# Second matrix of the second SwiGLU by seven block products, with operand sums made during the first matrix

## Chip, core and metric

The kernel runs on one core of one Trainium2 chip. The metric is the device time of one execution in microseconds, as the median of several runs.

## What is computed

The reference is a two-layer diffusion trunk: 1024 latent tokens and 256 context tokens of width 1024, a Fourier mixer in the first layer, differential attention in the second, and a SwiGLU behind each. Only the last SwiGLU is touched, over the 1024 latent tokens, all in float32:

```python
def swiglu(h, w_in, w_out):
    gate, up = jnp.split(h @ w_in, 2, axis=-1)
    return (jax.nn.silu(gate) * up) @ w_out

x = x + g2 * swiglu(modulate(rms_norm(x, norm_gain[i, 1]), sh2, sc2), ffn_w_in[i], ffn_w_out[i])
```

`w_in` is 1024 x 5632 (gate and up, 2816 columns each), `w_out` 2816 x 1024.

## The kernel before

Every float32 matmul is made of three in the float32r format: high times high, high times low and low times high (`mm3`, lines 49 to 52, or `prod`, lines 1447 to 1452). The operands are split beforehand: ScalarE copies the high part (line 55) and VectorE subtracts it for the low part (line 56). One such split of 128 x 512 numbers is called a unit.

The last SwiGLU has two stages.

The first matrix (lines 1369 to 1585) goes over the 2816 columns in 22 rows f of 128. Each row makes gate and up for both halves of the tokens (g = 0 and 1, 512 tokens each) from seven products instead of eight, numbered 1, 2, 5, 6, 3, 7, 4. A product is 4 x 3 matmuls of 128 x 128 by 128 x 512 into one PSUM bank. The order of the products is `seq`; from row 3 on a row's product 3 comes between products 6 and 7 of the next row. `load` fetches the weight columns of a row through SP's DMA queue, nine products ahead in the text (LEADL). `prep` makes the weight sums on GpSimd (lines 1435 to 1441) and splits them into units, four ahead (LEADP); there are six unit buffers. `evac` reads the banks out: line 1471 (ScalarE copies a bank), 1479 (VectorE adds the second product to the gate), 1480 and 1493 (silu on ScalarE), 1488, 1491 and 1497 (further VectorE sums with a bank). `act_out` multiplies gate and up on GpSimd (line 1463) in place in one of ten buffers e, writes the 128 x 512 result to `aD` in DRAM and frees both buffers.

The second matrix (lines 1588 to 1662) makes the output transposed: for each half g of the tokens eight banks, one for each 128 columns of `w_out`, take 22 steps f of 8 x 3 matmuls. `prep_down` loads a row of `w_out` (512 KB) and a half row of `aD` (256 KB) and splits both. Two steps are prepared during the first matrix (`load_first`, `prep_first`). In the last six steps of a half (TAIL) the loop runs bank by bank, so that a bank is finished, scaled and added to the residual `xt` on VectorE (line 1654) while the others still accumulate. `store` transposes finished columns on TensorE (line 1617), copies them out of PSUM through buffers o (line 1620) and writes them to the output. The residual halves are loaded from DRAM at lines 1598 and 1599; the tile xt0 has been used for weight columns of the first rows before.

The text gives each engine's operations in an order and with buffers by name; the program builder sets the waits and may move an operation ahead of others on its engine where its inputs and buffers allow it.

## Time and profile before

| | us |
|---|---|
| median of 3 runs | 2753.19 (2752.32 to 2753.29) |
| the profiled execution | 2754.87 |
| its span, first to last instruction | 2753.1 |
| first matrix of the last SwiGLU, first matmul to last | 2068 to 2500 |
| second matrix, first matmul to last | 2500 to 2747 |

The profile is of one execution. Engines: PE is TensorE's matmuls, PEld its weight loads, DVE is VectorE, ACT ScalarE, POOL GpSimd, SP the queue that issues the DMAs. L12 is line 12 of the kernel. Durations of matmuls overlap, so a matmul's price is the distance from one start to the next. In a timeline row stand the start, the duration, engine, line, operation, what it writes and reads, and in brackets how long the engine was idle before it and what ended that.

### The profile page before, as it was taken

Reading aid. Unit: us, or ns where it says so; the run is one execution under the profiler, and the core shown is the slowest. Engines: PE = TensorE matmul, PEld = TensorE weight load, DVE = VectorE, ACT = ScalarE, POOL = GpSimd, SP = SyncE. Lnnn points to the kernel's source line nnn. Section 1 sums busy time; section 2 is a strip of 40 time slices with the busy share of each in tenths; the row PEclk is TensorE's granted clock in tenths of the full one; section 3 lists DMA queues with packets and bytes.
Section 4 is the critical chain, followed back from the end, with each engine's and each line's share of the span. In section 5 each row is a group of like instructions: output and inputs, shape, how many; then the busy total and the mean of one; then the engine's idle time right before and its main releaser. Section 6 shows DMA issues by size and latency. Waiting matters only on the chain. (4 is left out here: it accounts for less than half of the span.)

```text
span 2753.1 us, 35789 instructions
## 1 busy us (share of the span) xinstructions
PE 2658.3 (97%) x13242; PEld 2185.4 (79%) x13242; DVE 1544.1 (56%) x2867; ACT 1118.4 (41%) x1954; POOL 952.1 (35%) x786
## 2 busy tenths in 40 slices
PE   6999999999999999999999899998988999999999
PEld 3678888888888888878888677787776788888887
DVE  6744535443344343485776597898458555554242
ACT  4643333323232111242444488898444333334131
POOL 4332023312121000022333287888145666651000
PEclk9999999999999999999999999999999999999999
DMA  6583122223232111133344632423243323226352
GB/s 213 190 270 100 39 62 82 88 74 95 73 96 70 39 35 43 53 105 105 115 146 144 197 105 70 123 85 100 81 137 107 103 73 88 73 85 214 103 184 88
DMA packets 288641, 292.75 MB, mean 106 GB/s; under 512 B 16313, under 2 KB 206034, under 8 KB 288466
## 3 DMA queue, kind: packets, MB, share of 16 engines
q1 hardware_dynamic: 286306, 286.79, 33.7%
q0 software_dynamic: 2160, 3.67, 0.4%
q8 instruction: 104, 1.70, 0.3%
q14 instruction: 71, 0.58, 0.1%
HBM read 236.93 MB, written 53.48 MB: 105 GB/s over the span
## 5 line engine op out<-in xcount | busy, mean ns | idle before, releaser
L50 PE MATMUL ps<-un,whl 128*128 128x512 f32 x1184 | 465.1, 394 | 1.4 <-ACT XT L602 1.2
L51 PE MATMUL ps<-un,whl 128*128 128x512 f32 x1184 | 462.1, 390 | 0.2 <-DVE un L56 0.2
L52 PE MATMUL ps<-un,whl 128*128 128x512 f32 x1184 | 461.4, 390 | 0.0
L56 DVE TENSOR_TENSOR whl<-raw,whl 128x512 fp32r<-128x512 f32 x219 | 169.7, 787 | 267.6 <-ACT whl L55 266.5
L50 PEld LDWEIGHTS ps<-un,whl 128*128 128x128 f32 x1184 | 222.7, 188 | 55.1 <-issue 3.5
L52 PEld LDWEIGHTS ps<-un,whl 128*128 128x128 f32 x1184 | 222.7, 188 | 47.1
L51 PEld LDWEIGHTS ps<-un,whl 128*128 128x128 f32 x1184 | 222.9, 188 | 45.1 <-DVE un L56 0.7
L55 ACT ACTIVATE whl<-raw 128x512 fp32r<-128x512 f32 x219 | 134.3, 627 | 243.8 <-PE ps L52 177.9
L746 DVE SCALAR_TENSOR_TENSOR XT<-ps,mods,XT 128x512 f32<-128x512 f32 (+1 forms) x264 | 170.2, 659 | 84.7 <-PE ps L52 84.7
L272 POOL TENSOR_TENSOR acc<-acc,aw 128x512 f32<-128x512 f32 x84 | 113.1, 1346 | 295.0 <-ACT acc L268 231.7
L1051 POOL TENSOR_TENSOR e<-e,e 128x1280 f32<-128x1280 f32 x62 | 183.4, 2961 | 32.1 <-ACT e L1050 29.9
L617 POOL TENSOR_TENSOR nacc<-nacc,s 128x512 f32<-128x512 f32 (+1 forms) x35 | 41.2, 1176 | 416.7 <-ACT s L616 395.2
L1031 ACT ACTIVATE e<-e,st 128x1280 f32<-128x1280 f32 x128 | 175.2, 1372 | 23.6 <-DVE e L1030 22.0
L1029 DVE TENSOR_SCALAR_CACHE_REDUCE e<-sc 128x1024 f32<-128x1024 f32 x128 | 155.3, 1219 | 28.4 <-POOL e L1051 14.1
L51 PE MATMUL ps<-u,whl 128*128 128x256 f32 x592 | 167.5, 283 | 0.0
L52 PE MATMUL ps<-u,whl 128*128 128x256 f32 x592 | 167.4, 283 | 0.0
L50 PE MATMUL ps<-u,whl 128*128 128x256 f32 x592 | 167.3, 283 | 0.0
L829 PE MATMUL ps<-whl,un 128*128 128x512 f32 x384 | 152.7, 398 | 0.0
L830 PE MATMUL ps<-whl,un 128*128 128x512 f32 x384 | 150.3, 392 | 0.9 <-DVE whl L56 0.7
L831 PE MATMUL ps<-whl,un 128*128 128x512 f32 x384 | 149.9, 391 | 0.0
L51 PE MATMUL b<-au,wu 128*128 128x512 f32 x336 | 130.9, 390 | 0.2 <-DVE au L56 0.2
L52 PE MATMUL b<-au,wu 128*128 128x512 f32 x336 | 130.8, 389 | 0.0
(447 smaller groups left out, 6380.5 us busy)
## 6 DMA issues: line engine op xcount, KB each, us to landing
aw<-in_w_ada SPq DMA_DIRECT2D x96, 256.0 KB, 2.8
raw<-in_ffn_w_in SPq DMA_DIRECT2D x88, 256.0 KB, 2.9
wr<-in_ffn_w_out SPq DMA_DIRECT2D x42, 512.0 KB, 3.6
wada<-in_w_ada SPq DMA_DIRECT2D x48, 256.0 KB, 3.2
un<-in_w_ada SPq DMA_DIRECT2D x48, 256.0 KB, 4.6
raw<-in_diff_w_in SPq DMA_DIRECT2D x48, 256.0 KB, 3.5
rq<-in_ffn_w_in SPq DMA_DIRECT2D x24, 512.0 KB, 5.7
raw<-in_ffn_w_out SPq DMA_DIRECT2D x44, 256.0 KB, 2.9
```

The source lines that it names most:

```text
L50: PE.matmul(out, wh, mh, start=start, stop=False)
L51: PE.matmul(out, wh, ml, start=False, stop=False)
L52: PE.matmul(out, wl, mh, start=False, stop=stop)
L55: S.activation(out=hl[:, 0], in_=src, func=AF.Copy)
L56: (lo_eng or V).tensor_tensor(out=hl[:, 1], in0=src, in1=r32(hl[:, 0]), op=ALU.subtract)
L746: V.scalar_tensor_tensor(out=xs, in0=pt, scalar=gmod[c][:, nn:nn + 1], in1=xs, op0=ALU.mult, op1=ALU.add)
L829: PE.matmul(pt, hk[:, 0, tsl], ws[k][:, 0], start=k == 0, stop=False)
L830: PE.matmul(pt, hk[:, 0, tsl], ws[k][:, 1], start=False, stop=False)
L831: PE.matmul(pt, hk[:, 1, tsl], ws[k][:, 0], start=False, stop=k == NC - 1)
L1029: V.tensor_scalar(e[:, 0:L], sc.rearrange("p a b -> p (a b)"), -1.0, 3.0e38, op0=ALU.mult, op1=ALU.min, accum_out=col(c))
L1031: S.activation(out=e, in_=e, func=AF.Exp, scale=-1.0, bias=col(4 + c), accum_out=col(10 + c))
L1051: G.tensor_tensor(out=e0, in0=e0, in1=e1, op=ALU.add)
```

## The change

Rows f of the first matrix are paired: an even row 2i makes row i of the upper half of the 2816, an odd row 2i + 1 row i of the lower half (`row`). So each pair gives four activation blocks, b11 and b12 (upper, both halves of the tokens) and b21 and b22 (lower). The second matrix is now seven products of half size in place of eight, each over 11 rows, four blocks of 128 columns and 512 tokens: 1, 2 and 4 take plain blocks of `w_out`, 3, 5, 6 and 7 sums of them (`sD` in DRAM), and the activations are plain blocks for 1, 2 and 3 and sums for 4 to 7 (`bD`).

The sums are made in `sums`, called by `act_out` when both halves of a row are there: one subtraction on VectorE after an even row, followed by the loads of four blocks of `w_out`; seven additions and subtractions after an odd row, followed by seven DMA writes. From row 4 on `act_out` writes its result into half of the tile xt0 (`side_tile`), not into an e buffer; the weight blocks take the other half. In the first four rows the results stay in e buffers until the pair is done.

The second matrix runs the products in groups (1, 2), (5, 6), (3, 7), (4), with TAIL = 4. `down_evac` spreads each product over the outputs it belongs to. Three units' products, (1, 0), (2, 0) and (1, 1), are prepared in the first matrix. The o buffers are three in place of four, and the last stores are in another order.

```diff
--- before.py
+++ after.py
@@ -1368,8 +1368,15 @@
     ph5.close()
     ph6 = ExitStack()
     wp = ph6.enter_context(tc.tile_pool(name="wp6", bufs=1, reuse_waits="tile"))
-    aD = dram.tile([NF, P, L], F32, name="aD")
+
+    NH = NF // 2
+    bD = {k: dram.tile([NH, P, 512], F32, name=f"bD{k}") for k in (1, 2, 3, 4, 5, 6, 7)}
+    sD = {k: dram.tile([NH, P, 512], F32, name=f"sD{k}") for k in (3, 5, 6, 7)}
     EARLYF, LEADP, LEADL, OWN, NB = 3, 4, 9, 2, 10
+
+    def row(f):
+
+        return f // 2 + NH * (f % 2)
     efree = list(range(NB))
     def eget():
@@ -1391,6 +1398,7 @@
     def wcols(c0):
         return w_in[:, c0:c0 + P].rearrange("(k p) n -> p k n", p=P)
+    w_out = a["ffn_w_out"][1]
     raws, units, again = {}, {}, []
     def load(f, i):
@@ -1398,7 +1406,7 @@
         if i == 1 and f < EARLYF:
             r = wp.tile([P, 1024], F32, name="r4", bufs=2) if f > 1 else \
                 hpool.tile([P, 2, 512], F32, name=f"h{18 + f}").rearrange("p s n -> p (s n)")
-            nc.sync.dma_start(r.rearrange("p (k n) -> p k n", k=NC), wcols(f * P))
+            nc.sync.dma_start(r.rearrange("p (k n) -> p k n", k=NC), wcols(row(f) * P))
             raws[f, "gate"] = r
         elif i == (1 if f >= EARLYF else 5):
             if 0 < f < EARLYF:
@@ -1409,14 +1417,14 @@
                 q = kq.tile([P, 2, 1024], F32, name="rq", tag="q")
                 r = [q[:, j] for j in range(2)]
             for j in range(2):
-                nc.sync.dma_start(r[j].rearrange("p (k n) -> p k n", k=NC), wcols(j * DFF + f * P))
+                nc.sync.dma_start(r[j].rearrange("p (k n) -> p k n", k=NC), wcols(j * DFF + row(f) * P))
             raws[f] = r
         elif i == 3 and 0 < f < EARLYF:
             if f == 1:
                 again.append(xt0_tile())
             r = [again[0][:, 4 * f + 2 * j - 4:4 * f + 2 * j - 2].rearrange("p a n -> p (a n)") for j in range(2)]
             for j in range(2):
-                nc.sync.dma_start(r[j].rearrange("p (k n) -> p k n", k=NC), wcols(j * DFF + f * P))
+                nc.sync.dma_start(r[j].rearrange("p (k n) -> p k n", k=NC), wcols(j * DFF + row(f) * P))
             raws[f, "again"] = r
     def prep(f, i):
@@ -1459,11 +1467,54 @@
             where[f] = bget()
         prod(where[f][1], units.pop((f, i)), held[i], i in (1, 2, 5, 4))
+    acts, side = {}, []
+
+    def side_tile(k):
+        if not side:
+            side.append(xt0_tile())
+        return side[0][:, k]
+
     def act_out(f, g, e, other):
-        G.tensor_tensor(out=e[1], in0=e[1], in1=other[1], op=ALU.mult)
+        i, odd = divmod(f, 2)
+        keep = f < 4
+        dst = e[1] if keep else side_tile(4 + 2 * odd + g)
+        G.tensor_tensor(out=dst, in0=e[1], in1=other[1], op=ALU.mult)
         eput(other)
-        nc.sync.dma_start(aD[f, :, g * 512:(g + 1) * 512], e[1])
-        eput(e)
+        if not keep:
+            eput(e)
+        acts[i, odd, g] = dst, e if keep else None
+        if (odd, g) != (0, 1):
+            nc.sync.dma_start(bD[{(0, 0): 1, (1, 0): 2, (1, 1): 3}[odd, g]][i], dst)
+        if (i, odd, 0) in acts and (i, odd, 1) in acts:
+            sums(i, odd)
+
+    def sums(i, odd):
+
+        def sub(out, in0, in1, op=ALU.subtract):
+            V.tensor_tensor(out=out, in0=in0, in1=in1, op=op)
+
+        x = [side_tile(k) for k in range(4)]
+        b11, b12 = acts[i, 0, 0][0], acts[i, 0, 1][0]
+        if not odd:
+            sub(b11, b12, b11)
+            nc.sync.dma_start(bD[5][i], b11)
+            for k, (r, c) in enumerate(((i, 0), (NH + i, 0), (i, 512), (NH + i, 512))):
+                nc.sync.dma_start(x[k], w_out[r * P:(r + 1) * P, c:c + 512])
+            return
+        b21, b22 = acts[i, 1, 0][0], acts[i, 1, 1][0]
+        sub(b12, b22, b12)
+        sub(b11, b22, b11)
+        sub(b21, b11, b21)
+        sub(x[3], x[2], x[3], ALU.add)
+        sub(x[2], x[0], x[2])
+        sub(x[0], x[3], x[0])
+        sub(x[1], x[1], x[0])
+        for d, ap in ((bD[7], b12), (bD[6], b11), (bD[4], b21), (sD[5], x[3]), (sD[7], x[2]), (sD[6], x[0]), (sD[3], x[1])):
+            nc.sync.dma_start(d[i], ap)
+        for m in range(4):
+            e = acts.pop((i, m // 2, m % 2))[1]
+            if e:
+                eput(e)
     def state(f):
@@ -1534,37 +1585,43 @@
         yield
-    w_out = a["ffn_w_out"][1]
-    FIRST = 2
     ups, drs = {}, {}
-
-    def load_first(f):
-        q = kq.tile([P, 2, 1024], F32, name="rq", tag="q")
-        nc.sync.dma_start(q[:, 0], w_out[f * P:(f + 1) * P, :])
-        nc.sync.dma_start(q[:, 1, 0:512], aD[f, :, 0:512])
-        drs[f] = q
-
-    def prep_first(f):
-        q = drs.pop(f)
-        us = [unit5(OWN) for _ in range(3)]
-        for u, src in zip(us, (q[:, 1, 0:512], q[:, 0, 0:512], q[:, 0, 512:1024])):
-            split(u, src)
-        ups[0, f] = us
+    FIRSTS = [(1, 0), (2, 0), (1, 1)]
+
+    def down_src(k, i):
+
+        r, c = {1: (i, 0), 2: (NH + i, 0), 4: (NH + i, 512)}.get(k, (None, None))
+        return sD[k][i] if r is None else w_out[r * P:(r + 1) * P, c:c + 512], bD[k][i]
+
+    def load_first(k, i):
+        drs[k, i] = [eget(), eget()]
+        for e, src in zip(drs[k, i], down_src(k, i)):
+            nc.sync.dma_start(e[1], src)
+
+    def prep_first(k, i):
+        us = []
+        for e in drs.pop((k, i)):
+            us.append(unit5(OWN))
+            split(us[-1], e[1])
+            eput(e)
+        ups[k, i] = us
     half = second_half()
     next(half)
     nload = nprep = 0
-    todo = seq + [("down", f) for f in range(FIRST)]
+    todo = seq + [("down", ki) for ki in FIRSTS]
     def ahead(n):
         nonlocal nload, nprep
         while nload < min(len(todo), n + LEADL):
             f, i = todo[nload]
-            load_first(i) if f == "down" else load(f, i)
+            if f == "down" and nload >= n + LEADP + 2:
+                break
+            load_first(*i) if f == "down" else load(f, i)
             nload += 1
         while nprep < min(len(todo), n + LEADP):
             f, i = todo[nprep]
-            prep_first(i) if f == "down" else prep(f, i)
+            prep_first(*i) if f == "down" else prep(f, i)
             nprep += 1
     ahead(0)
@@ -1590,24 +1647,27 @@
     psb = ph7.enter_context(tc.tile_pool(name="ps7", bufs=1, space=PSUM, reuse_waits="tile"))
     bfree[:] = range(8)
     out = a["out"].rearrange("o t d -> (o t) d")
-    TAIL = 6
+    TAIL = 4
     xt0 = xt0_tile()
     xt1 = [kq.tile([P, 4, 512], F32, name="xt1", tag="q") for _ in range(2)]
     xt = [xt0, Halves(xt1)]
     for k in range(0, NC, 4):
         nc.sync.dma_start(xt0[:, k:k + 4], x2[:, k:k + 4, 0:512])
         nc.sync.dma_start(xt1[k // 4], x2[:, k:k + 4, 512:1024])
-
-    def prep_down(g, f):
-        raw = wp.tile([P, 1024], F32, name="wr", bufs=3)
-        nc.sync.dma_start(raw, w_out[f * P:(f + 1) * P, :])
-        ar = t2("ar", 3)
-        nc.sync.dma_start(ar, aD[f, :, g * 512:(g + 1) * 512])
-        au = wp.tile([P, 2, 512], F32R, name="au", bufs=8)
-        split(au, ar)
-        w = wp.tile([P, 2, 1024], F32R, name="wu", bufs=6)
-        split(w, raw)
-        ups[g, f] = au, w[:, :, 0:512], w[:, :, 512:1024]
+    gm = mod(1, 0, 5)
+    ngm = wp.tile([P, 32], F32, name="ngm")[:, 0:NC]
+    V.tensor_scalar(ngm, gm, -1.0, None, op0=ALU.mult)
+    uacc = [wp.tile([P, 512], F32, name=f"ua{m}") for m in range(4)]
+
+    def prep_down(k, i):
+        us = []
+        for nm, src in zip(("w", "a"), down_src(k, i)):
+            raw = t2(nm + "r", 4)
+            nc.sync.dma_start(raw, src)
+            u = wp.tile([P, 2, 512], F32R, name=nm + "u", bufs=11)
+            split(u, raw)
+            us.append(u)
+        ups[k, i] = us
     def store(g, k0, k1):
         for j in range(4):
@@ -1615,51 +1675,82 @@
             pb = bget()
             for k in range(k0, k1):
                 PE.transpose(out=pb[1][:, (k - k0) * P:(k - k0 + 1) * P], in_=xt[g][:, k, tsl], identity=ident)
-            o = t2("o", 4)
+            o = t2("o", 3)
             n = (k1 - k0) * P
             (S.copy if j % 2 else V.tensor_copy)(out=o[:, 0:n], in_=pb[1][:, 0:n])
             bput(pb)
             nc.sync.dma_start(out[g * 512 + j * P:g * 512 + (j + 1) * P, k0 * P:k1 * P], o[:, 0:n])
-    stream = [(g, f) for g in range(2) for f in range(NF) if (g, f) not in ups]
+    GROUPS = ((1, 2), (5, 6), (3, 7), (4,))
+    stream = [(k, i) for ks in GROUPS for i in range(NH) for k in ks]
+    stream = [ki for ki in stream if ki not in ups]
     at = 0
     def ahead_down(n):
         nonlocal at
-        while at < min(len(stream), n - FIRST):
+        while at < min(len(stream), n - len(FIRSTS)):
             prep_down(*stream[at])
             at += 1
-    ahead_down(4)
-    for g in range(2):
-        acc = []
-
-        def step(f, nn):
-            au, *ws = ups[g, f]
-            w = ws[nn // 4]
-            nsl = slice((nn % 4) * P, (nn % 4 + 1) * P)
-            mm3(acc[nn][1], w[:, 0, nsl], w[:, 1, nsl], au[:, 0], au[:, 1], f == 0, f == NF - 1)
-
-        for f in range(NF - TAIL):
-            for nn in range(NC):
-                if f == 0:
-                    acc.append(bget())
-                step(f, nn)
-            ahead_down(g * NF + f + 4)
-        ahead_down((g + 1) * NF)
-        for nn in range(NC):
-            for f in range(NF - TAIL, NF):
-                step(f, nn)
-            xs = xt[g][:, nn]
-            V.scalar_tensor_tensor(out=xs, in0=acc[nn][1], scalar=mod(1, 0, 5)[:, nn:nn + 1], in1=xs, op0=ALU.mult, op1=ALU.add)
-            bput(acc[nn])
-            if nn == 1:
-                ahead_down((g + 1) * NF + 3)
-            if g == 1 and nn in (2, 3):
-                store(0, 4 * (nn - 2), 4 * (nn - 1))
-            if g == 1 and nn in (4, 6):
-                store(1, *((0, 4), (4, 6))[nn // 2 - 2])
-    store(1, 6, 8)
+    def add(g, d, src, neg=False):
+        xs = xt[g][:, d]
+        V.scalar_tensor_tensor(out=xs, in0=src, scalar=(ngm if neg else gm)[:, d:d + 1], in1=xs, op0=ALU.mult, op1=ALU.add)
+
+    def down_evac(k, m, pt):
+        u = uacc[m]
+        if k == 1:
+            S.activation(out=u, in_=pt, func=AF.Copy)
+        elif k == 2:
+            add(0, m, pt)
+            add(0, m, u)
+        elif k == 5:
+            add(1, m, pt)
+            add(1, 4 + m, pt)
+        elif k == 6:
+            V.tensor_tensor(out=u, in0=u, in1=pt, op=ALU.add)
+        elif k == 3:
+            add(1, m, pt)
+            add(1, m, u)
+        elif k == 7:
+            V.tensor_tensor(out=u, in0=u, in1=pt, op=ALU.add)
+            add(0, 4 + m, u)
+            add(1, 4 + m, u)
+        else:
+            add(0, 4 + m, pt, neg=True)
+
+    acc = {}
+
+    def step(k, m, i):
+        if i == 0:
+            acc[k, m] = bget()
+        w, au = ups[k, i]
+        nsl = slice(m * P, (m + 1) * P)
+        mm3(acc[k, m][1], w[:, 0, nsl], w[:, 1, nsl], au[:, 0], au[:, 1], i == 0, i == NH - 1)
+
+    base = 0
+    ahead_down(8)
+    for ks in GROUPS:
+        for i in range(NH - TAIL):
+            for k in ks:
+                for m in range(4):
+                    step(k, m, i)
+            ahead_down(base + (i + 1) * len(ks) + 8)
+        for k in ks:
+            for m in range(4):
+                for i in range(NH - TAIL, NH):
+                    step(k, m, i)
+                down_evac(k, m, acc[k, m][1])
+                bput(acc.pop((k, m)))
+                if ks == (4,):
+                    if m in (0, 1):
+                        store(1, 4 * m, 4 * m + 4)
+                    if m == 2:
+                        store(0, 0, 4)
+                    if m == 3:
+                        store(0, 4, 6)
+            ahead_down(base + len(ks) * (NH - TAIL) + 8 + (TAIL * (ks.index(k) + 1)))
+        base += NH * len(ks)
+    store(0, 6, 8)
     ph7.close()
     phq.close()
     up3.close()
```

## Rows read from the trace of the kernel before

**Rows 1.** The page's busy time, share of the span and instructions of TensorE.

```profile
PE 2658.3 (97%) x13242; PEld 2185.4 (79%) x13242; DVE 1544.1 (56%) x2867; ACT 1118.4 (41%) x1954; POOL 952.1 (35%) x786
```

**Rows 2.** Busy time of the engines in three stages, granted clock, DMA share, GB/s.

```profile
core 0: us, PE busy (x) PEld busy (x) DVE busy (x) ACT busy (x) POOL busy (x), PEclk, DMA share, GB/s
...
2150.00:2497.20 347.20, 347.20 (x1513) 283.85 (x1512) 184.39 (x198) 128.71 (x216) 217.45 (x157) 1.00 0.26 78
...
2497.20:2512.00 14.80, 14.72 (x64) 11.63 (x63) 3.97 (x6) 3.48 (x5) 3.01 (x2) 1.00 0.82 288
...
2512.00:2747.30 235.30, 235.11 (x1067) 194.98 (x1066) 91.39 (x108) 69.28 (x90) 0.00 (x0) 1.00 0.44 149
```

**Rows 3.** Timeline of TensorE in the second matrix; and the page's group.

```profile
L51 PE MATMUL b<-au,wu 128*128 128x512 f32 x336 | 130.9, 390 | 0.2 <-DVE au L56 0.2
...
2620.25 0.39 PE L50 MATMUL b<-au,wu 128*128 128x512 f32 x1
...
2630.45 0.39 PE L50 MATMUL b<-au,wu 128*128 128x512 f32 x1
```

**Rows 4.** VectorE in row f's end: a stretch's busy times, and timeline.

```profile
2322.48:2330.09 7.61, 7.61 (x35) 6.28 (x34) 5.18 (x6) 2.38 (x4) 7.45 (x6) 1.00 0.09 34
...
2318.39 0.69 DVE L1491 TENSOR_TENSOR e<-e,b 128x512 f32<-128x512 f32 x1 [0.94 <-PE b L1452]
...
2319.11 0.69 DVE L56 TENSOR_TENSOR whl<-e,whl 128x512 fp32r<-128x512 f32 x1
...
2322.48 1.74 DVE L56 TENSOR_TENSOR whl<-e,whl 128x512 fp32r<-128x512 f32 x1
...
2329.40 0.69 DVE L1479 TENSOR_TENSOR e<-e,b 128x512 f32<-128x512 f32 x1 [0.52 <-PE b L1452]
```

**Rows 5.** Timeline of GpSimd in the same row.

```profile
2321.14 1.28 POOL L1463 TENSOR_TENSOR e<-e,e 128x512 f32<-128x512 f32 x1
...
2323.63 1.74 POOL L1435 TENSOR_TENSOR e<-rq 128x512 f32<-128x512 f32 x1
```

**Rows 6.** Timeline of ScalarE in the same row.

```profile
2330.12 0.63 ACT L1480 ACTIVATE e<-e 128x512 f32<-128x512 f32 x1
...
2334.99 0.60 ACT L1471 ACTIVATE e<-b 128x512 f32<-128x512 f32 x1 [2.10 <-PE b L1452]
```

**Rows 7.** Groups by line, 2150 to 2490: busy us, mean ns, idle before.

```profile
L56 DVE TENSOR_TENSOR wo<-e,wo 128x512 fp32r<-128x512 f32 x45 | 47.9, 1064 | 41.7 <-ACT wo L55 41.2
```

**Rows 8.** First rows: timeline of GpSimd and TensorE, and a stretch's busy times.

```profile
2131.65 1.25 POOL L1463 TENSOR_TENSOR e<-e,e 128x512 f32<-128x512 f32 x1
...
2136.18 0.80 PE L1450 MATMUL b<-h,wo 128*128 128x512 f32 x1 [4.88 <-ACT wo L55]
...
2136.00:2140.00 4.00, 3.82 (x8) 2.65 (x9) 3.84 (x3) 1.69 (x4) 3.92 (x3) 0.50 1.06 350
```

**Rows 9.** Between the matrices: timeline of SP, ScalarE, TensorE; and a DMA issue.

```profile
2121.12 0.37 SPq L1598 DMA_DIRECT2D xt<-x  x1
...
2503.09 0.32 SPq L1465 DMA_DIRECT2D aD<-e  x1
...
2503.45 0.43 SPq L1603 DMA_DIRECT2D wr<-in_ffn_w_out  x1
...
2509.70 1.06 ACT L55 ACTIVATE wu<-wr 128x1024 fp32r<-128x1024 f32 x1 [8.00 <-DMA wr<-in_ffn_w_out]
...
2512.68 0.50 PE L51 MATMUL b<-au,wu 128*128 128x512 f32 x1 [0.19 <-DVE au L56]
...
ar<-aD SPq DMA_DIRECT2D x42, 256.0 KB, 3.6
```

**Rows 10.** The end: TensorE's last matmul; DMA issues, KB each, us to landing.

```profile
2746.84 0.39 PE L52 MATMUL b<-au,wu 128*128 128x512 f32 x1
...
out<-o SPq DMA_DIRECT2D x12, 256.0 KB, 2.5
...
out<-o SPq DMA_DIRECT2D x8, 128.0 KB, 1.8
```

## The prediction

> **What bounds the kernel now.** I began with the page's busy shares: TensorE holds 97% of the span [rows 1], so the question is whether each stage is TensorE's to the last microsecond. The table by stage answers it [rows 2]. In the first matrix's steady part (2150 to 2497.2 us) TensorE is busy 347.20 of 347.20 us while VectorE has 53% and GpSimd 63%. In the second matrix (2512 to 2747.3) it is busy all but 0.2 of 235.3 us, GpSimd does nothing, and the DMA engines are at 44%. So a matmul taken out of the second matrix is worth its full pitch, provided nothing else becomes late. The third view is the timeline, for that pitch and for the slack of the other engines.
>
> A busy time per matmul (390 ns in the page) isn't its price, since matmuls overlap. Start to start, 45 matmuls lie between the two L50 rows: 2630.45 - 2620.25 = 10.20 us, or 0.2267 us each [rows 3].
>
> **Removed: an eighth of the second matrix.** Before: 44 steps (g, f) of 8 x 3 matmuls, 1056 in all (336 per line in the row, three lines, and 48 for the two early steps [rows 3]). After: 7 products x 11 rows x 4 x 3 = 924. That is 132 x 0.2267 = 29.9 us less. The 64 transposes of the stores are the same. Gain: **-29.9 us**.
>
> **Second matrix, the rest of its steady part: 0.** A unit of 12 matmuls lasts 2.72 us. It needs two loads of 256 KB, 524 KB in 2.72 us, or 193 GB/s; now it is 149 on average, and 288 were moved in the busiest stage [rows 2]. Two splits cost VectorE and ScalarE under 1.4 us each (0.69 and about 0.63 a piece [rows 4, 6]). Evictions grow from 16 to 44 VectorE operations, at most three (about 2.25 us) in the 2.72 us of one tail step. A tail holds eight units of eleven, so three are ready when the next group starts, and four more can be prepared in its second half. TensorE hides all that; were the loads to lack a tenth of their time, 77 units would cost 21 us, but the row of 288 speaks against it.
>
> **Added to the first matrix: eight subtractions or additions per pair of rows, on VectorE.** They come as one after an even row and seven in a run after an odd one, as soon as GpSimd has made the second activation (L1463). In capacity there is room: 8 x 0.69 = 5.5 us in the 38.7 us of a pair. What matters is what stands behind the run. GpSimd's product ends at 2322.42 [rows 5]. From 2322.48 to 2330.09, the end of the gate sum L1479, VectorE is busy 5.18 of 7.61 us, so it has 2.43 us to spare [rows 4]. Behind L1479 ScalarE waits for its silu (L1480, 0.63), then does a split (0.63) and the copy of the sixth product (L1471, 0.60, at 2334.99) [rows 6]; the seventh product adds to that bank, one product later. Four products lie between the ends L1491 and L1479 answer to: 11.01 us, 2.75 each [rows 4]. So the copy may end at 2334.99 + 2.75 = 2337.7, L1479 at 2337.7 - 1.86 = 2335.8, which is 5.7 us later than now. With a price p for each of the seven, TensorE is held up by 7p - 2.43 - 5.7. Prices: 0.69 for a split that meets no GpSimd work, 1.74 for one that does [rows 4], 1.064 as the mean of 45 [rows 7]. At 0.69 and 1.064 there is no stall (the second leaves 0.7 us); at 1.74 it is 4.05 us, in nine steady pairs 36 us. GpSimd is busy 7.45 of those 7.61 us [rows 4], so I go a little above the mean, p = 1.23, or 0.48 us a pair: **+4 us (0 to 36)**. Weight units are split some four products ahead, 11 us, and come through a run of 8.6 us. GpSimd gives back what it loses in its idle third.
>
> The row first: beside a GpSimd addition the VectorE split took 1.74 us instead of 0.69, and the GpSimd operation next to it 1.74 instead of 1.28, while VectorE operations with one input in PSUM keep 0.69 [rows 4, 5]. The Trainium skill (SBUF — State Buffer, "Who interferes with whom") has a rule for it: a VectorE instruction with two SBUF inputs and a GpSimd instruction that reads SBUF exclude each other for the whole instruction, whichever came first. All eight added operations have two SBUF inputs. By that rule alone each waits out a GpSimd operation, which is the 1.74 price and the rival "port" below.
>
> **The DMAs of the first matrix** (seven writes of activations for the four before, four of weight sums, four loads of weight rows per pair) add 15 x 256 KB less 4 x 256 KB, 2.9 MB in 38.7 us or 75 GB/s to 78 [rows 2]. They share SP's queue with the loads of the first matrix. These would stand behind up to 12 us of writes waiting for VectorE, and are issued more than a row (19 us) ahead. Cost 0; without that cover it would be the excess over 19 us, a pair at a time.
>
> **The first rows: +2 us (-7 to +12).** Here GpSimd is the chain, TensorE waits 4.88 us until 2136.18, and in the next 4 us its granted clock is 0.50, the 1.2 GHz level: eight matmuls in 3.82 us, 0.48 each [rows 8]. The order of GpSimd's queue is the program builder's, and the change moves it. It also holds the activations of rows 0 to 3 in the ten e buffers: after the seventh product of row 2, three middle sums, three up sums and three activations, nine of ten, where now six are held. A run of seven at the dear price is 12.2 us; if the new order loses the wait, 4.88 + 8 x (0.48 - 0.23) = 7 us come back. I take a small loss: the run becomes ready when the L1463 of 2131.65 ends [rows 8], beside the very GpSimd work that TensorE waits for.
>
> **Between the matrices: +3 us (0 to 12).** Two steps of 24 matmuls were prepared early (10.9 us); now three units of 12 (8.2 us). The first streamed matmul, 0.19 us late at 2512.68 [rows 9], is then due near 2509. The loads for it are issued at 2503.45, right behind the last write that waits for GpSimd (2503.09) [rows 9]. If that stays, they land 3.6 us later [rows 9], and two splits (0.63 + 0.63 + 0.69) make 2509.0: no stall, the last run of seven (2503.1 to 2507.9 with GpSimd idle) having just left VectorE. If they stand behind its seven writes, they start at 2508, and the stall is 4.6 us. There is more: the residual xt0 is loaded now as early as 2121.12 [rows 9], which also shows that engines don't keep the order of the text. Its tile now holds the sums up to the last write, so 2 MB are loaded here. Were they in front of the units, these would wait for a write to land (2.5 [rows 10]) and take the 6.25 us of the first load now (2503.45 to 2509.70 [rows 9]): near 2518.5, a stall of 9.5 us and 2 at the lower clock. I take 3.
>
> **The end: +4 us (+1 to +6).** After the last matmul (2746.84 [rows 10]) 8 transposes remain now; after the change 16, another 1.0 us, and eight copies go through three o buffers instead of four. A buffer comes back only when its store has landed, 1.8 us for 128 KB, 2.5 for 256 KB [rows 10]. Two more rounds of copy, issue and landing, 0.4 + 0.4 + 1.8 = 2.6 us, begin before the old end; the stores of 1 MB just before leave about one round over. Between 1.0 and two rounds (5.2), I take 4.
>
> **Sum.** -29.9 + 4 + 2 + 3 + 4 = -16.9 us. The profiled execution took 2754.87 us (span 2753.1 and 1.8 around it), 1.7 above the median of 2753.19; the sum goes to both, 2738.0 for a profiled one and **2736.3** for the median.
>
> **Rivals.**
> "Hidden": everything beside the end is covered. 2753.2 - 29.9 + 3 = 2726. For it: no capacity is exceeded, and 5.7 us of slack. Against: four places must all come out well. 0.22.
> "Port" (slower than before): each subtraction waits for a GpSimd operation, p = 1.74, and the seventh product waits in every odd row. 2753.2 - 29.9 + 36 + 9 = 2768. It is a loss against before from (29.9 - 9)/9 = 2.3 us a pair, p = 1.49. For it: GpSimd is 98% busy where the run falls. Against: the mean over the stage is 1.064, and the run itself outlasts GpSimd's stretch. 0.11.
> "Drained": the units stand behind the sums' writes and xt0, and the first rows take a full run: 2753.2 - 29.9 + 4 + 12 + 12 + 4 = 2755. For it: the new dependence of xt0. Against: xt0 isn't needed until the second product's tail, and loads that are ready went first before. 0.12.
> "Not as said": the count of matmuls doesn't fall to 924, because part is repeated or a load waits for all writes of a DRAM tile: no gain, 2753 or above. 0.03.
> The forecast, 2736 within 9 us: 0.52.
>
> **How the numbers follow.** Measurement can tell about 0.2% (5.5 us) from no change. Forecast and "hidden" are faster, with a bit of the others: 0.77. Within 0.2% (2747.7 to 2758.7) fall most of "drained" and the weak half of "port": 0.13. Slower: 0.10. The range runs from under "hidden" (2726 less some of the early gain) to just over "drained": 2723 to 2757. "Port" and a full gain in the first rows are left out.
>
> **What would show it.** In the trace after: 924 matmuls of the second matrix at lines 50 to 52, at an unchanged pitch of 0.2267 us; the second matrix some 28 us shorter; TensorE without waits in the first matrix, or a wait for the copy L1471 in every second row ("port"); the subtractions at 0.7 to 1.7 us with a mean near 1.2; one wait for a split where the matrices meet; after the last matmul 10 us instead of 6.3. Wrong would be: a gain under 10 us with no waits in these four places, or a pitch that rises in the second matrix because loads land late.

## The result, and the profile after

The changed kernel takes 2778.05 us (2775.61 to 2780.36) where the kernel before takes 2752.76: the ratio is 1.0095 [1.0077, 1.0112]. It is slower by 25 us, against a forecast of 17 us faster and a range that ended at 2757. The profiled execution took 2777.78 us, with a span of 2775.8. Run again beside the experiments below, the kernel before took 2750.47 and 2750.66 us (medians), which is how far its own median moves.

In the new numbering L1494 is all the sums, L1502 their loads of `w_out`, L1513 their writes, L1481 the product of gate and up (before L1463), L1522 the copy of a bank (L1471), L1530 and L1542 VectorE's sums with a bank (L1479, L1491), L1531 and L1544 the silus (L1480, L1493), L1487 the write of an activation (L1465). In the experiments the numbers shift by a line or a few: L1523 and L1518 there are the copy of a bank, L1514 the writes of the sums. A table made from the first and last starts of the matmuls of each stage says where the time is. The first matrix is counted from the start of its seventh product to its last matmul, here and in the 2068 to 2500 given for the kernel before: the first six products (1 and 2 of rows 0 to 2) are made earlier, from 2040.0 us on before and from 2042.1 after. The second matrix is counted from there to its last matmul, the end from there to the last instruction.

| us | start of the first matrix | first matrix | second matrix | end | span |
|---|---|---|---|---|---|
| before | 2068.0 | 431.9 | 246.9 | 6.3 | 2753.1 |
| after | 2070.5 | 468.8 | 226.1 | 10.4 | 2775.8 |
| difference | +2.5 | **+36.9** | **-20.8** | +4.1 | +22.7 |

The second matrix gains as it should, apart from a wait at its beginning. The loss is in the first matrix, and there in one part of it, as the table by stage shows (columns as in [rows 2]):

```profile
PE 2643.8 (95%) x13110; PEld 2169.4 (78%) x13110; DVE 1665.4 (60%) x3048; ACT 1134.9 (41%) x2022; POOL 963.6 (35%) x786
...
2139.00:2307.00 168.00, 141.04 (x562) 111.51 (x561) 112.85 (x129) 44.24 (x80) 86.42 (x60) 0.92 0.63 209
2320.00:2539.00 219.00, 219.00 (x954) 179.06 (x954) 147.19 (x152) 80.28 (x136) 142.19 (x98) 1.00 0.35 111
2539.00:2557.00 18.00, 9.38 (x40) 7.01 (x39) 4.24 (x8) 2.69 (x5) 1.72 (x2) 0.82 0.70 251
2557.00:2765.40 208.40, 208.40 (x936) 172.81 (x937) 126.59 (x196) 89.05 (x156) 0.00 (x0) 0.99 0.58 194
```

The kernel before kept TensorE busy without a gap from 2150 on [rows 2]. Now that is so from 2320 on, while from 2139 to 2307 TensorE is idle for 27 us, at a granted clock of 0.92, and the DMA engines are at 63%. What differs between the two stretches? The first three rows below are by source line (count, ns, first and last start), the fourth is the landing times of L1502; the last four are the waits of TensorE, VectorE and ScalarE from 2070 to 2560 (sum in us, times, longest).

```profile
L1502 SPq DMA_DIRECT2D xt<-in_ffn_w_out x44: 327/384/1136, 2129.0 to 2299.4; - x44
L1513 SPq DMA_DIRECT2D sD<-xt x44: 319/326/1105, 2140.8 to 2306.9; - x44
L1494 DVE TENSOR_TENSOR xt<-xt x80: 676/726/1790, 2139.0 to 2543.8; 128x512 f32<-128x512 f32 x80
DMA to landing us min/median/max: 2.8/3.9/5.7
...
PE b L1458 <- ACT e L1522: 30.2, 9, 6.7
...
DVE xt L1494 <- DMA xt<-in_ffn_w_out: 41.6, 9, 7.1
...
ACT e L1531 <- DVE e L1530: 55.2, 15, 9.8
ACT e L1544 <- DVE e L1542: 43.6, 9, 10.2
```

All 44 loads of weight blocks and all 44 writes of their sums are issued by 2307, while the activation sums go on to 2543.8. So the weight sums of all eleven pairs were not made pair by pair, but in (2306.9 - 2139.0)/11 = 15.3 us a round, where a pair of rows has 38.7. And VectorE stands 41.6 us, in nine waits, for those loads. One of them, in time order (start, duration, engine, line; in brackets how long the engine was idle and what ended it; the first row is SP's own wait between 2258 and 2272):

```profile
SPq L1487 <- POOL xt L1481: 4.9, 1, 4.9
...
2266.47 0.32 SPq L1487 DMA_DIRECT2D bD<-xt  x1
2266.84 0.91 SPq L1502 DMA_DIRECT2D xt<-in_ffn_w_out  x2
...
2270.11 0.69 DVE L1494 TENSOR_TENSOR xt<-xt 128x512 f32<-128x512 f32 x1 [6.07 <-DMA xt<-in_ffn_w_out]
2270.72 0.68 DVE L1530 TENSOR_TENSOR e<-e,b 128x512 f32<-128x512 f32 x1
2271.43 0.63 ACT L1531 ACTIVATE e<-e 128x512 f32<-128x512 f32 x1 [9.77 <-DVE e L1530]
2272.49 0.58 ACT L1522 ACTIVATE e<-b 128x512 f32<-128x512 f32 x1
2273.12 0.80 PE L1458 MATMUL b<-ot,wo 128*128 128x512 f32 x1 [6.67 <-ACT e L1522]
```

The load is issued at 2266.84, right behind the write of an activation (L1487) for which SP had stood 4.9 us, until GpSimd had made that activation; the load itself shows no wait. VectorE, which reached the sum 6.07 us earlier, goes on at 2270.11. The gate sum L1530 had been queued behind it. ScalarE's silu waits for that (9.77 us in all), the copy L1522 stands behind the silu, and TensorE waits 6.67 us for the copy, because its next product adds to that bank. It is the chain that the prediction worked out for a run of seven, set off by another cause: not the price of the sums but a DMA in front of one. In other waits of the nine the load goes out when the writes of the round before have landed and so have freed the buffer of four blocks (SP's waits of that kind are 16.4 us in sum from 2125 to 2320). So a hoisted load waits for its buffer or for SP's queue, and VectorE for the load.

### The profile page after: what moved, and what is told of

Read it like the earlier page. It is cut to its first block, busy times and chain, and to the rows that moved or that the text cites. A ratio compares the mean times of both kernels' runs of the same rounds, so it can differ in the third digit from the quotient of the medians.

```text
span 2775.8 us, 36267 instructions
## 1 busy us (share of the span) xinstructions
PE 2643.8 (95%) x13110; PEld 2169.4 (78%) x13110; DVE 1665.4 (60%) x3048; ACT 1134.9 (41%) x2022; POOL 963.6 (35%) x786
## 3 DMA queue, kind: packets, MB, share of 16 engines
q0 software_dynamic: 2160, 3.67, 0.4%
## 5 line engine op out<-in xcount | busy, mean ns | idle before, releaser
L50 PE MATMUL ps<-un,whl 128*128 128x512 f32 x1184 | 465.2, 394 | 1.4 <-ACT XT L602 1.2
L50 PEld LDWEIGHTS ps<-un,whl 128*128 128x128 f32 x1184 | 222.7, 188 | 55.3 <-issue 3.5
L1031 ACT ACTIVATE e<-e,st 128x1280 f32<-128x1280 f32 x128 | 175.2, 1372 | 24.3 <-DVE e L1030 22.7
L50 PE MATMUL ps<-u,whl 128*128 128x256 f32 x592 | 167.3, 283 | 0.0
L1494 DVE TENSOR_TENSOR xt<-xt 128x512 f32<-128x512 f32 x80 | 92.2, 1164 | 80.4 <-DMA xt<-in_ffn_w_out 41.6
L50 PE MATMUL b<-au,wu 128*128 128x512 f32 x296 | 116.3, 393 | 8.5 <-ACT au L55 8.5
```

What stands on the lines that cost most here:

```text
L50: PE.matmul(out, wh, mh, start=start, stop=False)
L1031: S.activation(out=e, in_=e, func=AF.Exp, scale=-1.0, bias=col(4 + c), accum_out=col(10 + c))
```

## The experiments

Three theories were to be told apart. "Hoisted" ("early weight sums" in the expectations): the weight sums depend on nothing but `w_out` and a buffer of four blocks, so they were put early, and VectorE stands for their loads. "Port", from the prediction: the sums meet GpSimd's work and are dear. "First rows": the e buffers that rows 0 to 3 hold are the loss. If "hoisted" holds, a second question is whether the wait for the loads alone is the loss, or the early place.

A single time cannot settle small differences here. The start of the first matrix lay between 2062.5 and 2070.5 in these ten kernels, which do the same work up to there. So stage lengths, counted from that start, are compared first, and medians where there are several runs. How well stage lengths repeat can be read from the four kernels below with the same paced first matrix: 439.8 to 440.0 us.

| us | first matrix | second | end | span | time |
|---|---|---|---|---|---|
| before | 431.9 | 246.9 | 6.3 | 2753.1 | |
| after | 468.8 | 226.1 | 10.4 | 2775.8 | |
| paced | 439.9 | 228.3 | 9.8 | 2746.0 | 2745.45 (median of 10) |
| one load | 457.2 | 227.0 | 10.4 | 2760.0 | 2761.82 (one) |
| no weight sums | 434.1 | 226.3 | 10.0 | 2739.2 | 2740.94 (one) |
| no activation sums | 477.5 | 224.2 | 9.8 | 2780.3 | 2782.23 (one) |
| paced, xt0 late | 439.8 | 221.1 | 10.4 | 2741.0 | 2742.09 (median of 4) |
| paced, stores early | 440.0 | 228.8 | 7.3 | 2739.4 | 2743.98 (median of 10) |
| paced, first rows free | 436.6 | 227.8 | 9.8 | 2736.7 | 2738.50 (one) |
| all three, last sums late | 439.9 | 217.8 | 7.4 | 2731.7 | 2735.00 (median of 5) |

**The weight sums held to their pair.** The same work; only the builder is told to issue the four weight sums after the pair's last activation sum. (`sub` returns its operation for this.)

```diff
-        sub(b21, b11, b21)
-        sub(x[3], x[2], x[3], ALU.add)
-        sub(x[2], x[0], x[2])
-        sub(x[0], x[3], x[0])
-        sub(x[1], x[1], x[0])
+        last = sub(b21, b11, b21)
+        with tc.issue_after(last.ins):
+            sub(x[3], x[2], x[3], ALU.add)
+            sub(x[2], x[0], x[2])
+            sub(x[0], x[3], x[0])
+            sub(x[1], x[1], x[0])
```

> The changed kernel with one rule of order more: the four weight sums of a pair stand on VectorE behind that pair's activation sums (the four operations, their loads and writes stay). Theory 'early weight sums': in the changed kernel all 44 weight sums were done between 2139 and 2307, ahead of their activations, each set waiting on VectorE for its four loads through one buffer (41.6 us of waiting), with the evictions and splits of the first matrix behind it. Paced, each set's loads have landed long before; the first matrix goes from 469 us (2070.5 to 2539.3) back to 432 to 440, and the time from 2778 to about 2741 to 2748. Rival 'port' (two-input VectorE operations against GpSimd): the same operations on the same engine, so at most 10 us come back, 2768 or more; TensorE then waits in every second row. Rival 'first rows' (four e buffers held): no change, 2775 to 2780.

2745.45 us against 2750.47 for the kernel before: a ratio of 0.9979 [0.997, 0.9989], or 0.2% faster. The first matrix is 28.9 us shorter than in the changed kernel. VectorE's wait for the weight loads falls from 41.6 us to 1.4 (its row in the list of L1494, second line below); the steady part from 2200 on runs at the full clock with short waits, of which two are shown.

```profile
L1494 DVE TENSOR_TENSOR xt<-xt x80: 676/1184/1785, 2138.2 to 2515.2; 128x512 f32<-128x512 f32 x80
  DMA xt<-in_ffn_w_out: 1.4, 1
...
PE b L1458 <- ACT e L1523: 14.2, 10, 6.6
...
2200.00:2507.00 307.00, 304.30 (x1318) 246.68 (x1317) 232.75 (x238) 108.46 (x189) 197.69 (x135) 1.00 0.49 160
...
2264.86 0.50 PE L1458 MATMUL b<-ot,wo 128*128 128x512 f32 x1 [0.48 <-ACT e L1523]
2304.21 0.50 PE L1458 MATMUL b<-ot,whl 128*128 128x512 f32 x1 [0.39 <-ACT e L1523]
```

"Hoisted" holds: same operations, loads and writes, and 28.9 of the 36.9 us lost in the first matrix are back. "Port" expected at most 10 us back and "first rows" none. With the sums, the loads and writes on SP move apart too; this run does not separate the order on VectorE from the order on SP. This run also shows the step that the prediction had sized for an odd row: one short wait in every second row, 0.32 to 0.48 us, for the copy of the sixth product.

**The weight rows loaded once.** The sums of the later pairs then work on what the first left; their loads are absent, everything else, the early place included, stays.

```diff
             for k, (r, c) in enumerate(((i, 0), (NH + i, 0), (i, 512), (NH + i, 512))):
-                nc.sync.dma_start(x[k], w_out[r * P:(r + 1) * P, c:c + 512])
+                if i == 0:
+                    nc.sync.dma_start(x[k], w_out[r * P:(r + 1) * P, c:c + 512])
```

> The changed kernel with the weight blocks loaded for the first pair only: the loads of the ten other pairs are left out (their sums are made of whatever the buffer holds), while all eight VectorE operations per pair and all DMA writes stay, and the weight sums still run early. Theory 'early weight sums', with the loads as what VectorE waits for: most of the 41.6 us is gone; a wait for the writes (2 to 4 us a set, 4 DMAs) can remain. First matrix 435 to 450 us, time 2743 to 2758. Rival 'port': the operations crowd together all the more, no gain, 2775 or above.

2761.82 us; the first matrix is 457.2, so only 11.6 of the 36.9 us come back. That is longer than the 435 to 450 expected. The wait for loads is gone by construction, but the sums are now even denser. First the writes of the weight sums, then a window by engines (busy time of TensorE, its weight loads, VectorE, ScalarE, GpSimd), the waits, and TensorE's longest:

```profile
L1514 SPq DMA_DIRECT2D sD<-xt x44: 319/320/1219, 2135.8 to 2223.3; - x44
...
2160.00:2180.00 20.00, 14.14 (x60) 11.19 (x60) 19.79 (x24) 3.68 (x7) 10.16 (x7) 1.00 0.59 223
...
DVE xt L1494 <- DMA sD<-xt: 6.6, 2, 6.1
...
2185.28 0.79 PE L1458 MATMUL b<-h,wo 128*128 128x512 f32 x1 [9.68 <-ACT e L1523]
```

Eleven rounds now take 87.5 us, 8.0 a round. In them VectorE is full (19.79 of 20.00 us from 2160 to 2180), GpSimd waits for its splits and ScalarE for its sums with a bank, and TensorE waits 27.1 us in six places before 2223 and nowhere after. So the loads are not the whole cause. Sums in the wrong place cost time with loads (standing) and without them (crowding); in their pair's place, with the loads, they cost 5.8 us (439.9 paced against 434.1 without any, in the next run). Whether a second buffer of blocks, or a queue of their own for the loads, would have been enough was not tried.

**No weight sums; no activation sums.** Two kernels that each leave out one half of the added work.

```diff
-        sub(x[3], x[2], x[3], ALU.add)
-        sub(x[2], x[0], x[2])
-        sub(x[0], x[3], x[0])
-        sub(x[1], x[1], x[0])
...
-            sub(b11, b12, b11)
-        sub(b12, b22, b12)
-        sub(b11, b22, b11)
-        sub(b21, b11, b21)
```

The first four lines, with the loads and writes that belong to them, are left out in the one, where the second matrix reads plain blocks of the weights instead, the last four alone in the other.

> The changed kernel without the weight sums: their loads, four VectorE operations and four writes per pair are left out, and products 3, 5, 6 and 7 read plain blocks of the weights instead. The four activation operations per pair stay. Theory 'early weight sums': first matrix 430 to 436 us, time about 2738 to 2744, a lower bound for what pacing can give. Rival 'port': half of the added operations remain, so about half of the 37 us: 2757 to 2762.

> The changed kernel without the four activation operations per pair (the activations are written unsummed); the weight sums, their loads and all writes stay. Theory 'early weight sums': nothing changes in the first matrix, 460 to 475 us, with VectorE waiting about 40 us for the weight loads, time 2770 to 2780. Rival 'port': half of the added operations gone, 2757 to 2762. Rival 'first rows' is not tested, as the buffers are held all the same.

Without the weight sums the time is 2740.94 us and the first matrix 434.1; TensorE waits 10.3 us in three places, all before 2178, and never in the steady part. Without the activation sums the time is 2782.23 us, and the first matrix, at 477.5, is no better than with all the sums. The waits of that second kernel, and its sums, which are now the weight sums alone:

```profile
L1494 DVE TENSOR_TENSOR xt<-xt x44: 677/693/1779, 2138.1 to 2307.8; 128x512 f32<-128x512 f32 x44
...
DVE xt L1494 <- DMA xt<-in_ffn_w_out: 50.2, 12, 9.9
...
PE b L1458 <- ACT e L1518: 40.2, 11, 8.0
```

Half of these sums cost 693 ns or less, the price of an operation that meets no GpSimd work, and the loss is there in full. That is the end of "port" as the cause: the dear price belongs to the activation sums, which fall beside GpSimd's work (alone, without the weight sums, they have a median of 1.76 us), and those cost the first matrix about 2 us (434.1 against 431.9).

**The load of xt0 moved into the second matrix** (with the sums paced).

```diff
     for k in range(0, NC, 4):
-        nc.sync.dma_start(xt0[:, k:k + 4], x2[:, k:k + 4, 0:512])
         nc.sync.dma_start(xt1[k // 4], x2[:, k:k + 4, 512:1024])
...
             ahead_down(base + (i + 1) * len(ks) + 8)
+            if ks == (1, 2) and i in (3, 5):
+                h = 4 * (i // 4)
+                nc.sync.dma_start(xt0[:, h:h + 4], x2[:, h:h + 4, 0:512])
```

> The paced kernel with the residual xt0 loaded in the fourth and sixth step of the second matrix's first group, not at its head. In the paced kernel TensorE waits 3.9 us for the first streamed unit and 5.2 us for the second, whose loads went out around the 2 MB of xt0. Theory 'drained between the matrices': the second wait goes, the first (loads behind the last sums' seven writes) stays: 4 to 7 us less than the paced kernel, about 2739 to 2741. Rival: the loads are late because of the seven writes alone, 0 to 1 us.

2742.09 us, a ratio of 0.9961 [0.9947, 0.9976] to before. The second matrix is 7.2 us shorter than paced alone, at the upper end of the 4 to 7 expected; the medians differ by 3.4. There TensorE waited at two places (first two rows: TensorE, paced); here at one (last row: its waits with xt0 late):

```profile
2520.89 0.79 PE L50 MATMUL b<-au,wu 128*128 128x512 f32 x1 [3.90 <-ACT au L55]
2530.69 2.07 PE L50 MATMUL b<-au,wu 128*128 128x512 f32 x4 [5.17 <-ACT au L55]
...
PE b L50 <- ACT au L55: 3.9, 1, 3.9
```

The 5.17 us were xt0's, in front of the second streamed unit. The other 3.9 us are not; in the paced kernel the seven writes of the last pair's sums are issued up to 2516.26, and the first streamed load right behind them, at 2516.35.

**The stores of finished halves before the last tail** (with the sums paced). In the last group three of the stores that waited until the tail come in its untailed steps, as their columns are complete.

```diff
             ahead_down(base + (i + 1) * len(ks) + 8)
+            if ks == (4,) and i in (1, 3, 5):
+                store(*((1, 0, 4), (1, 4, 8), (0, 0, 4))[i // 2])
...
-                if ks == (4,):
-                    if m in (0, 1):
-                        store(1, 4 * m, 4 * m + 4)
-                    if m == 2:
-                        store(0, 0, 4)
-                    if m == 3:
-                        store(0, 4, 6)
+                if ks == (4,) and m == 2:
+                    store(0, 4, 6)
```

> The paced kernel with three of the four large stores moved into the untailed steps of the last group, and the store of columns 4 and 5 ahead of the last block, so that only one store of 128 x 256 pieces follows the last matmul (as in the kernel before). Theory 'end': the time from the last matmul to the end falls from about 10 us to 6 to 6.5, so 3.5 to 4 us less than the paced kernel, about 2741 to 2742. Rival: the three o buffers set the end wherever the stores stand, 0 to 1 us.

2743.98 us, 0.9977 [0.9968, 0.9986] to before. The end is 7.3 us instead of 9.8, where 6 to 6.5 were expected. In the medians this is 1.5 us, within the spread of the two kernels.

**The first four rows without held results** (with the sums paced). Rows 0 to 3 give their e buffers back at once, and the sums of these two pairs are left out; plain blocks are written and read in their place.

```diff
+        if keep:
+            if (odd, g) == (0, 1):
+                nc.sync.dma_start(bD[5][i], dst)
+            if odd and g:
+                for d in (bD[7], bD[6], bD[4]):
+                    nc.sync.dma_start(d[i], dst)
+            eput(e)
+            return
```

> The paced kernel in which rows 0 to 3 keep no e buffer: their activation and weight sums are left out (the activations are written plain in their place, and the products read plain weight blocks there). In the paced kernel TensorE waits 6.6 us at 2132 and 3.5 us at 2179 for ScalarE's copy of a bank into an e buffer; before the change it waited 4.9 us in this stretch. Theory 'first rows, e buffers': the copy waits for a buffer that is kept, so both waits shrink to the 5 us of before or less, in sum 5 us or more with the clock. Rival 'first rows, work': the waits stand where GpSimd's queue is the chain, with or without kept buffers; the wait near 2132 stays at 4 to 7 us.

The waits of TensorE in the first rows, paced (first three rows) and here (last):

```profile
2132.49 0.79 PE L1458 MATMUL b<-h,wo 128*128 128x512 f32 x1 [6.62 <-ACT e L1523]
2142.31 0.50 PE L1458 MATMUL b<-ot,wo 128*128 128x512 f32 x1 [1.35 <-ACT e L1523]
2179.27 0.80 PE L1458 MATMUL b<-h,wo 128*128 128x512 f32 x1 [3.49 <-ACT e L1523]
...
2130.00 0.79 PE L1458 MATMUL b<-h,wo 128*128 128x512 f32 x1 [7.14 <-ACT wo L55]
```

Without held buffers and without early sums the wait near 2130 is still there, no shorter, and it has the releaser that it had in the kernel before (4.88 us, [rows 8]). So that wait is not made by the held buffers or by the first sums. The waits of 1.35 us near 2142 and 3.49 us near 2179 are gone, so those are theirs; in exchange two of 1.52 and 0.39 us near 2120 are there, as in the kernel before (1.52 and 0.40). The first matrix is 3.3 us shorter; the rest of the single time of 2738.50 is an early start (2062.5).

**All together, and the last pair's sums behind the first streamed units.** Paced, xt0 late, stores early; the sums of the last pair, which only later groups need, are issued in the second matrix after the second streamed unit's load and split (`marks` holds these two instructions of each unit).

```diff
-        if (i, odd, 0) in acts and (i, odd, 1) in acts:
+        if (i, odd, 0) in acts and (i, odd, 1) in acts and (i, odd) != (NH - 1, 1):
             sums(i, odd)
...
+            if ks == (1, 2) and i == 0:
+                with tc.issue_after(marks[1][0]), tc.issue_after(marks[1][1]):
+                    sums(NH - 1, 1)
```

> The paced kernel with xt0 late, the stores early, and the last pair's seven sums and writes behind the loads and splits of the second streamed unit. If the four places are independent: 2745.5 less 9 to 11 between the matrices and 4 at the end, 2731 to 2734, and faster than the kernel before by 0.6 to 0.75%. If the waits only move on (the next units late, or the sums of the last pair late for product 5), 2738 or above.

2735.00 us against 2750.66: a ratio of 0.9939 [0.9926, 0.9953], faster than both kernels by more than the noise, and 1 us above the 2731 to 2734 expected. The wait between the matrices is down to 0.9 us:

```profile
PE b L1458 <- ACT e L1523: 13.8, 10, 5.4
...
PE b L50 <- ACT au L55: 0.9, 1, 0.9
```

The second matrix is 217.8 us, 29.1 less than before. That the 3.9 us left by the late xt0 stood behind the last pair's sums fits this, though nothing else was tried for it.

## Why the prediction was wrong, step by step

**Removed: right.** The pitch is unchanged at 194 GB/s of DMA where it was 149: 45 matmuls from one L50 row to another again take 2650.13 - 2639.93 = 10.20 us [rows 2, 3]. Once the wait at its beginning is gone, the second matrix is shorter by 29.1 us, of a predicted 29.9. In the changed kernel it is 20.8 shorter; the wait of 8.54 us treated below is the rest. "The rest of its steady part: 0" is right too: 208.40 of 208.40 us busy.

**"They come as one after an even row and seven in a run after an odd one, as soon as GpSimd has made the second activation": this step failed.** It holds for the activation sums, whose input is that activation, and fails for the four weight sums, which take nothing from the row. The size of what it left out is the 36.9 us of the first matrix, against a predicted 6. Of these, 28.9 come back when the weight sums are held to their pair. With it fell "The DMAs of the first matrix ... Cost 0": that step asked only whether the loads of the first matrix come late behind SP's writes, and had no line for the new loads. In their early place these do come late, for their buffer or for SP (which stood 4.9 us for GpSimd in front of the load at 2266.84), and the sum is queued on VectorE before they land. The wait on the path was VectorE's, the one engine for which the DMA step had no line. The prediction held the clue in its hand: it read from the row of xt0 at 2121.12 that engines don't keep the order of the text [rows 9], and used it for the residual alone.

Why the builder gives these sums that place in VectorE's queue no trace shows; that they are there, and that holding them back undoes 28.9 us, is shown. The Trainium skill (PSUM — Partial Sum Buffer, "Engine vs sequencer instructions") says that the queues of VectorE and ScalarE are strictly first in, first out; the gate sum at 2270.72 behind the weight sum at 2270.11 agrees.

**The price of a sum and the stall in odd rows: right, by way of the paced kernel.** p was taken as 1.23 us as the mean of a run of seven; the seven that begin at 2327.91 below take 1.22 us each on average, the single ones from 0.68 to 1.78. The stall was worked out as 0.48 us a pair, and the waits are 0.32 to 0.48 in every second row, seven of them, 14.2 - 6.62 - 1.35 - 3.49 = 2.7 us in sum where 4 was predicted. The picture behind it was not exact. In the paced kernel's VectorE timeline the seven don't run without a break: other operations stand among them (here L1540, a sum with a bank that is L1488 in the kernel before, after two). The gate sum, here L1531, does come behind the last of the seven, as the prediction had it:

```profile
2327.91 3.46 DVE L1494 TENSOR_TENSOR xt<-xt 128x512 f32<-128x512 f32 x2 [2.66 <-POOL xt L1481]
2331.30 0.68 DVE L1540 TENSOR_TENSOR e<-e,b 128x512 f32<-128x512 f32 x1
2331.89 1.28 DVE L1494 TENSOR_TENSOR xt<-xt 128x512 f32<-128x512 f32 x2
...
2337.71 1.78 DVE L1494 TENSOR_TENSOR xt<-xt 128x512 f32<-128x512 f32 x1
...
2341.12 0.67 DVE L1531 TENSOR_TENSOR e<-e,b 128x512 f32<-128x512 f32 x1
```

Two sums beside GpSimd take 3.46 us, two others 1.28. So the rule of the Trainium skill (SBUF — State Buffer, "Who interferes with whom") agrees with the price of single operations, and the rival that follows from it, every sum at 1.74 and a time of 2768, does not occur: the sums that are dear hold up TensorE by less than half a microsecond a pair.

**The first rows: too small.** +2 was predicted. The paced kernel has 6.62 + 1.35 + 3.49 = 11.46 us of waits there against 4.88 and three smaller ones of 1.19, 1.52 and 0.40 before, so 3.5 us more. The 1.35 and 3.49 are due to what rows 0 to 3 hold and sum, as supposed. Why the wait near 2130 is between 5.37 and 7.14 in the kernels with the change, and 4.88 before, is open: it stays when held buffers and early sums are taken away.

**Between the matrices: +3 was predicted, 8.5 came; "drained" was right here.** That rival had the units stand behind the sums' writes and xt0, and rejected it because loads that are ready went first before. The rows of SP and TensorE in the changed kernel:

```profile
2543.19 1.65 SPq L1513 DMA_DIRECT2D bD<-xt  x3
2546.66 0.92 SPq L1655 DMA_DIRECT2D xt<-x  x2
2547.67 0.45 SPq L1666 DMA_DIRECT2D wr<-in_ffn_w_out  x1
...
2556.87 0.80 PE L50 MATMUL b<-au,wu 128*128 128x512 f32 x1 [8.54 <-ACT au L55]
```

The 2 MB of xt0 wait from 2544.84 to 2546.66, until the last writes from its tile have landed (the page gives 2.0 us from issue to landing), and the first streamed loads stand behind them on SP. TensorE stands 8.54 us; the working in the prediction had 9.5.

**The end: right.** +4 was predicted, +4.1 came (10.4 us against 6.3), and five of VectorE's and ScalarE's last eight copies wait 0.9 to 1.4 us each for an o buffer whose store is landing, three of them here:

```profile
2768.15 0.42 DVE L1680 COPY o<-b 128x256 f32<-128x256 f32 x1 [1.25 <-DMA out<-o]
2769.76 0.42 DVE L1680 COPY o<-b 128x256 f32<-128x256 f32 x1 [1.18 <-DMA out<-o]
...
2772.02 0.37 ACT L1680 COPY o<-b 128x256 f32<-128x256 f32 x1 [1.12 <-DMA out<-o]
```

**The sum once more.** With the sums in the place that the prediction gave them, the paced kernel's span differs from before by +8.0 + (228.3 - 246.9) + 3.5 = -7.1 us, to a predicted -16.9. The 9.8 between them are 6.1 of the two waits between the matrices (9.1 to a predicted 3), 2.0 in the first matrix and 2.2 of the second matrix that no wait shows, less 0.5 at the end. With all repairs the time of 2735.00 is within 2 us of the forecast. That is chance and confirms nothing: it is another kernel, and the terms differ, the end and the place between the matrices being better than forecast, the first rows worse.

## What to carry to other kernels

Ask of every added operation what its own inputs are. One whose inputs are ready far ahead of the place where the text has it doesn't stay there: its loads and it may be queued as early as its buffer allows, and on an engine that keeps the order of its queue everything behind it then waits for its DMA. Before pricing such work, look for the thing that holds it to its place (an input made there, or an explicit order), and give each added DMA two lines in the working: who waits behind it in its queue, and which engine's queue holds its reader.

A load that is not needed soon should not be placed, in the text, ahead of loads that are needed at once, if it has to wait for something itself; the queue waits with it.

## What was not expected of the hardware

Waits of under half a microsecond did not lower TensorE's granted clock here, and one of several microseconds did. With waits of 0.32 to 0.48 us every 39 us the granted clock stays 1.00, the 2.4 GHz level, from 2200 to 2507 in the paced kernel. In the changed kernel a stretch of 20 us without a wait and one with the wait of 6.67 us show it (columns as above; the last row is the tenth matmul after the one that ended this wait at 2273.12):

```profile
2200.00:2220.00 20.00, 20.00 (x89) 16.34 (x88) 11.68 (x13) 5.06 (x9) 8.50 (x6) 1.00 0.60 197
...
2260.00:2280.00 20.00, 12.65 (x45) 9.93 (x46) 11.09 (x16) 6.08 (x12) 10.21 (x8) 0.83 0.73 223
...
2277.55 0.40 PE L1459 MATMUL b<-ot,wo 128*128 128x512 f32 x1
```

A mean of 0.83 means that a third of the stretch was granted the 1.2 GHz level. Behind the wait ten matmuls take 2277.55 - 2273.12 = 4.43 us from start to start, where ten at the pitch of 0.2267 take 2.27: this wait cost 2.2 us more than its own length. Of the 36.9 us lost in the first matrix, 27.8 are waits (42.1 us in sum, against 14.3 in the kernel before); the other 9 are not. Stretches like this one fit them, with a granted clock of 0.96 over the first matrix against 0.98 before, but they were not added up one by one.

The second matrix, at 194 GB/s on one core, keeps the matmul pitch of 0.2267 us. In the stretch of the hoisted sums, at 209 GB/s, a 256 KB load of weight blocks took 2.8 to 5.7 us to land.
